# TensorE's instructions in the loop over the mixers' tiles, in the order in which the code writes them

## The chip, the cores and the metric

The kernel runs on one core of a Trainium2 chip. The metric is the device time of one execution in microseconds (us), and the median of several runs is compared. The core has five engines with a queue each: TensorE (PE in the profile; PEld is its weight loads), VectorE (DVE), ScalarE (ACT), GpSimd (POOL) and SyncE (SP), which issues the DMAs here.

## The reference, cut to what matters

One layer of a streaming encoder on 1024 prompt frames and 32 sample frames, with model width 1024: a SwiGLU block, two attention mixers side by side, another SwiGLU block. This case is about the mixers.

```python
def band_attn_a(q, k, v, bias, valid):            # mixer A: 8 heads of 64, 576 keys for each chunk of 64
    s = jnp.einsum('bnqhd,bnkhd->bnhqk', q, k).astype(jnp.float32) * SCALE + bias.astype(jnp.float32)
    s = jnp.where(valid[None, :, None], s, NEG_INF)
    p = jax.nn.softmax(s, axis=-1).astype(v.dtype)
    return jnp.einsum('bnhqk,bnkhd->bnqhd', p, v)
...
o = jnp.concatenate([rmsnorm(oa, group_gains[:WIDTH_A]), rmsnorm(ob, group_gains[WIDTH_A:])], axis=-1) @ w_out
```

Mixer B has 8 query heads on 2 key heads, a window of 192 keys and a learned sink in the softmax. The sample frames attend to cached keys and values.

## The kernel before, in words

Tokens are in three blocks (384, 384, 256 + 32 columns). The first SwiGLU block runs, then the mixers, then the second one. The mixers' stage is a loop over 72 tiles (lines 1229 to 1262), which takes some 407 us of the 2220.7 us span. Tiles 0 to 35 are mixer B (four pairs of heads, each a sample tile `TileS` and eight tiles `TileB` of 128 queries), 36 to 53 are mixer A's pairs of heads 0 and 1, and 54 to 71 its pairs 2 and 3, taken in turn and beginning with those of few keys (128 keys for the first, 640 from the fifth on).

A tile of mixer A has two halves, one for each head. `qk` computes the scores `S` in PSUM with two matmuls (L766, L767): queries and keys are each split into a value rounded to the fast fp32 format (`F32R`) and what is left, and GpSimd makes the split queries `qs` (L738, L739) a tile ahead. Then DVE adds the bias (L769) and finds the maximum (L773), ACT takes the exponential `P` (L781). `tr` transposes `P` on TensorE into `pp` (L798), which ACT or DVE copies out as `PT`; `av` multiplies by the values into `po` (L724; for pairs 2 and 3 also two matmuls on `rden`, L718), which is copied out as `o`. A tile of mixer B is the same with both heads at once: `Sb` (L835, L836), DVE L837 and L839, ACT L846, a scaling (ACT L852, DVE L854), `ppb` (L864), `po`. A sample tile has `Ss`, `Ps`, `pps`, `po`.

PSUM has two buffers for scores (pool `ps2`), three for `pp`, `ppb` and all projections (`ps1`), one for `po` (`psc`).

Beside the tiles the loop runs other work on TensorE: the projections `pq` and `pv` of later heads (24 matmuls each in two pieces, by `fill`), `pkr` and `pkc` (transposed keys), the sums `pss` and `pr` of the group norms (`step`), and from tile 67 on five pieces `wo` of the output projection (`out_piece`). In which order the code writes this is plain from the body of the loop:

```python
for half in range(2):
    scores(n, half)
    tiles[n].tr(half)
    if half == 0 and n:
        tiles[n - 1].av()
    step(1)
    prep_step()
    fill(rate)
```

`scores(n, half)` writes the scores of tile n + 2 up to tile 35, of tile n + 1 from 36 on. The order in which instructions stand in the engines' queues is another matter: a scheduler sets it when the program is built. It takes, by its own estimate of times, what is ready first. `tc.manual_schedule(engines={...})` makes it keep the code's order on the engines named, for what is written inside the block. Buffers and semaphores follow the order that results.

Of the kernel before, what the change touches and what calls it, by code (L numbers as in the profile page):

```python
# [61 lines left out]
KB = 0  # L62
SPLIT = "ggg"
LEAD_B = 2
MANUAL = False
WAIT = 3
PREP = 3
STAGES = ((0, 34), (37, 54))
# [7 lines left out]
def encoder_step(ctx: ExitStack, tc, x_prompt, x_sample, cache_a_k, cache_a_v, cache_b_k, cache_b_v,  # L76
# [1183 lines left out]

    with tc.manual_schedule(engines={mybir.EngineType.PE}) if MANUAL else ExitStack():
        waits[0] = WAIT
# [121 lines left out]
```

## Time and profile before

| | |
|---|---|
| median of 3 runs | 2223.67 us (2222.75 to 2224.6) |
| the profiled execution | 2222.49 us, its span 2220.7 us |
| TensorE busy in the span | 2149.3 us (97%) |
| the other engines | DVE 1218.1 us, ACT 676.3 us, POOL 304.4 us |
| TensorE's mean granted clock | 0.984 |

A span is the time from the first instruction to the last. Matmuls are pipelined, so that a duration in the trace is longer than the time that a matmul takes from the next: a 128x384 matmul is listed with 0.33 us, and the next one starts 0.17 us later. What an instruction costs TensorE is read from starts, not from durations.

### The profile page before, as it was taken

Reading aid. Unit: us, or ns where it says so; the run is one execution under the profiler, and the core shown is the slowest. Engines: PE = TensorE matmul, PEld = TensorE weight load, DVE = VectorE, ACT = ScalarE, POOL = GpSimd, SP = SyncE. Lnnn points to the kernel's source line nnn. Section 1 sums busy time; section 2 is a strip of 40 time slices with the busy share of each in tenths; the row PEclk is TensorE's granted clock in tenths of the full one; section 3 lists DMA queues with packets and bytes.
Section 4 is the critical chain, followed back from the end, with each engine's and each line's share of the span. In section 5 each row is a group of like instructions: output and inputs, shape, how many; then the busy total and the mean of one; then the engine's idle time right before and its main releaser. Section 6 shows DMA issues by size and latency. Waiting matters only on the chain.

```text
span 2220.7 us, 34363 instructions
## 1 busy us (share of the span) xinstructions
PE 2149.3 (97%) x14092; PEld 2074.6 (93%) x14092; DVE 1218.1 (55%) x2314; ACT 676.3 (30%) x1391; POOL 304.4 (14%) x601
## 2 busy tenths in 40 slices
PE   6999999999999999899999899999999999999998
PEld 4999999999999999788788688999999999999998
DVE  5787667865333487566555675775333333333336
ACT  4411111111122253465555663443111111111133
POOL 2100000000000022455323633220000000000000
PEclk9999999999999999899999899999999999999999
DMA  9343334433212352110112121424211111111122
GB/s 323 101 142 115 113 96 124 143 92 112 64 58 70 100 182 81 57 39 21 49 40 60 39 86 67 133 82 117 73 57 39 54 43 38 58 39 57 39 68 80
DMA packets 200753, 186.06 MB, mean 84 GB/s; under 512 B 7724, under 2 KB 169940, under 8 KB 199444
## 3 DMA queue, kind: packets, MB, share of 16 engines
q1 hardware_dynamic: 200596, 183.87, 27.1%
q8 instruction: 110, 1.80, 0.3%
q14 instruction: 47, 0.39, 0.1%
HBM read 164.12 MB, written 22.86 MB: 84 GB/s over the span
## 4 chain that ended last, share of the span: by engine, by line
PE 86%; DVE 6%; DMA 3%; ACT 2%; issue 1%; POOL 1%; SPq 0%; DVEq 0%; ACTq 0%; POOLq 0%
PE dn L329 7%; PE dn L330 7%; PE dn L331 7%; PE gate L330 7%; PE up L330 7%; PE gate L331 7%; PE up L329 7%; PE up L331 7%; PE gate L329 7%; PE po L724 2%; PE pq L329 2%; PE pq L330 2%; PE pq L331 2%; PE pv L675 1%; PE pp L798 1%
## 5 line engine op out<-in xcount | busy, mean ns | idle before, releaser
L307 ACT ACTIVATE w<-raw 128x1024 fp32r<-128x1024 f32 x187 | 196.6, 1058 | 550.2 <-PE gate L330 227.3
L329 PE MATMUL gate<-h_hi,w 128*128 128x384 f32 (+1 forms) x1056 | 341.0, 323 | 4.4 <-DVE sl L555 2.9
L329 PE MATMUL dn<-gg,w 128*128 128x384 f32 (+1 forms) x1056 | 341.7, 325 | 2.3 <-DVE facc L585 2.3
L330 PE MATMUL gate<-h_lo,w 128*128 128x384 f32 (+1 forms) x1056 | 340.5, 322 | 3.5 <-DVE h_lo L450 3.5
L585 DVE TENSOR_TENSOR facc<-dn,facc 128x768 f32<-128x768 f32 (+1 forms) x240 | 212.5, 887 | 233.8 <-PE dn L331 233.8
L331 PE MATMUL gate<-h_hi,w 128*128 128x384 f32 (+1 forms) x1056 | 340.3, 322 | 0.0
L329 PE MATMUL up<-h_hi,w 128*128 128x384 f32 (+1 forms) x1056 | 340.1, 322 | 0.0
L330 PE MATMUL up<-h_lo,w 128*128 128x384 f32 (+1 forms) x1056 | 340.1, 322 | 0.0
L331 PE MATMUL up<-h_hi,w 128*128 128x384 f32 (+1 forms) x1056 | 339.8, 322 | 0.0
L330 PE MATMUL dn<-gg,w 128*128 128x384 f32 (+1 forms) x1056 | 339.8, 322 | 0.0
L331 PE MATMUL dn<-gg,w 128*128 128x384 f32 (+1 forms) x1056 | 339.2, 321 | 0.0
L308 DVE TENSOR_TENSOR w<-raw,w 128x1024 fp32r<-128x1024 f32 x187 | 231.4, 1245 | 129.7 <-ACT w L307 124.5
L372 POOL TENSOR_TENSOR sq<-sq 128x384 f32<-128x384 f32 (+1 forms) x48 | 51.9, 1091 | 1476.7 <-ACT sq L368 1468.3
L555 DVE TENSOR_TENSOR sl<-sl,up 128x384 f32<-128x384 f32 (+1 forms) x132 | 68.3, 518 | 309.4 <-PE up L331 303.6
L329 PEld LDWEIGHTS gate<-h_hi,w 128*128 128x128 f32 x1056 | 198.8, 188 | 5.3 <-DVE sl L555 3.2
L330 PEld LDWEIGHTS gate<-h_lo,w 128*128 128x128 f32 x1056 | 198.8, 188 | 4.1 <-DVE h_lo L450 4.0
L329 PEld LDWEIGHTS dn<-gg,w 128*128 128x128 f32 x1056 | 199.1, 189 | 3.6 <-DVE facc L585 3.5
L330 PEld LDWEIGHTS dn<-gg,w 128*128 128x128 f32 x1056 | 198.9, 188 | 0.1
L331 PEld LDWEIGHTS up<-h_hi,w 128*128 128x128 f32 x1056 | 198.9, 188 | 0.0
L331 PEld LDWEIGHTS gate<-h_hi,w 128*128 128x128 f32 x1056 | 198.9, 188 | 0.0
L330 PEld LDWEIGHTS up<-h_lo,w 128*128 128x128 f32 x1056 | 198.7, 188 | 0.0
L331 PEld LDWEIGHTS dn<-gg,w 128*128 128x128 f32 x1056 | 198.7, 188 | 0.0
(234 smaller groups left out, 3470.7 us busy)
## 6 DMA issues: line engine op xcount, KB each, us to landing
raw<-in_w_mod_dram SPq DMA_DIRECT2D x56, 512.0 KB, 4.0
raw<-in_w_gate_dram SPq DMA_DIRECT2D x54, 512.0 KB, 3.9
raw<-in_w_up_dram SPq DMA_DIRECT2D x54, 512.0 KB, 6.3
raw<-in_w_down_dram SPq DMA_DIRECT2D x54, 512.0 KB, 5.0
raw<-in_w_in_dram SPq DMA_DIRECT2D x18, 512.0 KB, 3.9
wm<-in_w_mod_dram SPq DMA_DIRECT2D x16, 512.0 KB, 6.6
raw<-in_w_out_dram SPq DMA_DIRECT2D x13, 512.0 KB, 4.3
xr<-xs SPq DMA_DIRECT2D x16, 384.0 KB, 5.0
```

The source lines that it names most:

```text
L307: ae.activation(w[0], r, AF.Copy)
L308: ve.tensor_sub(w[1], r, w[0])
L329: te.matmul(ps, w[0][:, k], hi, start=start, stop=False)
L330: te.matmul(ps, w[0][:, k], lo, start=False, stop=False)
L331: te.matmul(ps, w[1][:, k], hi, start=False, stop=stop)
L372: e.tensor_tensor(sq[:, 0, :w], sq[:, 0, :w], sq[:, 1, :w], op=OP.add)
L555: ve.tensor_tensor(sl[:, :w], sl[:, :w], ps[1][:, :w], op=OP.mult)
L585: ve.tensor_tensor(o, ps[:, :, :w], o, op=OP.add)
L675: te.matmul(ps[:n, :256], b, wt[0][:, kk], start=False, stop=k == KT - 1)
L724: te.matmul(po[64 * h:64 * h + 64, :n], vsl(j, h, kn), PT(h, j, kn), start=j == 0, stop=j == nt - 1)
L798: te.transpose(pp[:, j - j0, :], P[:, 128 * j:128 * j + 128], ident)
```

## The change

One constant, which decides whether the loop over the tiles is inside a manual schedule of TensorE.

```diff
 LEAD_B = 2
-MANUAL = False
+MANUAL = True
 WAIT = 3
```

It is used in one place, the line ahead of the loop:

```python
with tc.manual_schedule(engines={mybir.EngineType.PE}) if MANUAL else ExitStack():
```

The other engines' instructions stay the scheduler's to order. TensorE's rows before the loop stand as they did.

The first place is on TensorE near the end of mixer A's pair 1, around the ten `po` of one tile. Before:

```order
L767 MATMUL S<-KS,qs 128x320
L724 MATMUL po<-PT,vt 64x128
L766 MATMUL S<-KS,qs 128x320
L767 MATMUL S<-KS,qs 128x320
L766 MATMUL S<-KS,qs 128x320
L767 MATMUL S<-KS,qs 128x320
L1024 MATMUL pkr<-twice,KS 128x64 x8
L798 MATMUL pp<-ident,P 128x128 x4
L724 MATMUL po<-PT,vt 64x128 x2
L798 MATMUL pp<-ident,P 128x128
L724 MATMUL po<-PT,vt 64x128 x7
```

The same tile's rows with the change, on TensorE:

```order
L766 MATMUL S<-KS,qs 128x320
L767 MATMUL S<-KS,qs 128x320
L766 MATMUL S<-KS,qs 128x320
L767 MATMUL S<-KS,qs 128x320
L798 MATMUL pp<-ident,P 128x128 x5
L724 MATMUL po<-PT,vt 64x128 x10
L1031 MATMUL pkr_12053<-ident,KQs 32x128
```

The ten `po` of a tile stood in three pieces, with scores and transpositions between them; they stand in one piece now. (An fp32 matmul such as `po` is one row here and two instructions in the trace.) Over the whole loop `po` stands in 108 pieces before and in 73 after: 38 and 35 in mixer B's tiles, 39 and 19 in mixer A's pairs 0 and 1, 12 and 8 in the tiles of up to 512 keys that follow, 19 and 11 in the rest.

The second place is on TensorE where mixer A's pairs 2 and 3 begin with tiles of few keys, and the first group norm's sum `pss` is formed. Before:

```order
L766 MATMUL S<-KS,qs 128x128
L767 MATMUL S<-KS,qs 128x128
L724 MATMUL po<-PTs,aux 64x32 x8
L724 MATMUL po<-PTs,vs 64x32 x2
L766 MATMUL S<-KS,qs 128x256
L718 MATMUL po<-ident,rden 64x128 x2
L724 MATMUL po<-PT,vt 64x128
L766 MATMUL S<-KS,qs 128x256
L767 MATMUL S<-KS,qs 128x256 x2
L361 MATMUL pss<-ones,sq 128x1 x3
L798 MATMUL pp<-ident,P 128x128 x3
L724 MATMUL po<-PT,vt 64x128
```

The same place on TensorE with the change:

```order
L724 MATMUL po<-PTs,aux 64x32 x8
L724 MATMUL po<-PTs,vs 64x32 x2
L361 MATMUL pss<-ones,sq 128x1 x3
L766 MATMUL S<-KS,qs 128x128
L767 MATMUL S<-KS,qs 128x128
L798 MATMUL pp<-ident,P 128x128
L766 MATMUL S<-KS,qs 128x256
L767 MATMUL S<-KS,qs 128x256
L798 MATMUL pp<-ident,P 128x128
L718 MATMUL po<-ident,rden 64x128 x2
L724 MATMUL po<-PT,vt 64x128 x2
L766 MATMUL S<-KS,qs 128x256
```

The sum `pss` stood behind three more score tiles and stands ahead of them now; scores and transpositions take turns, one by one.

The third place is on TensorE at the first piece `wo` of the output projection, whose 24 matmuls read the normed outputs `o_hi` and `o_lo`. Before:

```order
L329 MATMUL wo<-o_hi,w 128x384
L798 MATMUL pp<-ident,P 128x128 x5
L718 MATMUL po<-ident,rden 64x128 x2
L724 MATMUL po<-PT,vt 64x128 x10
L330 MATMUL wo<-o_lo,w 128x384
L331 MATMUL wo<-o_hi,w 128x384
```

The same piece on TensorE with the change:

```order
L767 MATMUL S<-KS,qs 128x320
L798 MATMUL pp<-ident,P 128x128 x5
L329 MATMUL wo<-o_hi,w 128x384
L330 MATMUL wo<-o_lo,w 128x384
L331 MATMUL wo<-o_hi,w 128x384
```

The transpositions and the `po` that stood between the first matmul, on `o_hi`, and the second, on `o_lo`, have gone elsewhere; the second follows the first at once.

## Rows read from the trace of the kernel before

**Rows 1.** The page's busy time of each engine and TensorE's granted clock in 40 slices

```profile
PE 2149.3 (97%) x14092; PEld 2074.6 (93%) x14092; DVE 1218.1 (55%) x2314; ACT 676.3 (30%) x1391; POOL 304.4 (14%) x601
...
PEclk9999999999999999899999899999999999999999
```

**Rows 2.** The loop in four stretches: length, busy us of each engine, clock, DMA

```profile
924.00:1076.00 152.00, 147.90 (x1146) 131.33 (x1147) 92.11 (x283) 88.98 (x308) 74.40 (x211) 0.99 0.11 30
1076.00:1222.00 146.00, 140.68 (x1022) 122.21 (x1020) 79.83 (x191) 74.33 (x186) 41.91 (x130) 0.98 0.20 53
1222.00:1261.00 39.00, 30.01 (x201) 22.26 (x199) 26.95 (x86) 22.72 (x65) 26.89 (x63) 0.78 0.18 51
1261.00:1331.00 70.00, 67.80 (x555) 60.08 (x553) 49.52 (x129) 45.65 (x97) 31.75 (x66) 1.00 0.23 69
```

**Rows 3.** TensorE's waits for `po`'s copy in the loop: total us, times, longest

```profile
PE po L718 <- DVE o L729: 2.8, 3, 1.3
```

**Rows 4.** TensorE's timeline at pieces of `po`: start, duration

```profile
1199.33 0.31 PE L767 MATMUL S<-KS,qs 128*128 128x320 f32 x1
1199.57 0.43 PE L724 MATMUL po<-PT,vt 128*64 128x128 f32 x2
1199.93 0.42 PE L766 MATMUL S<-KS,qs 128*128 128x320 f32 x1
1200.18 0.31 PE L767 MATMUL S<-KS,qs 128*128 128x320 f32 x1
1200.33 0.31 PE L766 MATMUL S<-KS,qs 128*128 128x320 f32 x1
...
1209.47 0.44 PE L724 MATMUL po<-PT,vt 128*64 128x128 f32 x4
1209.84 0.33 PE L798 MATMUL pp<-ident,P 128*128 128x128 f32 x1
1210.10 1.09 PE L724 MATMUL po<-PT,vt 128*64 128x128 f32 x14
...
1267.18 0.44 PE L718 MATMUL po<-ident,rden 128*64 128x128 f32 x4 [1.27 <-DVE o L729]
...
1268.42 0.41 PE L766 MATMUL S<-KS,qs 128*128 128x320 f32 x1
```

**Rows 5.** DVE and ACT in the loop by form: what follows mixer B's scores

```profile
L837 DVE TENSOR_TENSOR Sb<-Sb,bias 128x512 f32<-128x512 f32 x28 | 19.6, 699 | 18.1 <-PE Sb L836 17.7
L839 DVE TENSOR_REDUCE nmb<-Sb 128x2 f32<-128x512 f32 x28 | 19.2, 684 | 0.3
...
L846 ACT ACTIVATE Pb<-Sb,nmb 128x256 f32<-128x256 f32 x56 | 26.0, 472 | 5.1 <-DVE nmb L840 4.2 <-DVE denb L849 0.9
L852 ACT ACTIVATE Pb<-Pb,denb 128x256 f32<-128x256 f32 x28 | 14.1, 505 | 5.4 <-DVE denb L849 5.0
```

**Rows 6.** Timeline of TensorE and ACT where mixer A begins

```profile
1077.29 0.66 PE L724 MATMUL po<-PTb,vt 128*64 128x128 f32 x8
1081.21 0.48 PE L766 MATMUL S<-KS,qs 128*128 128x128 f32 x1 [3.27 <-ACT Ps L910]
...
1082.69 0.69 PE L924 MATMUL pps<-ident,Ps 64*128 64x64 f32 x4 [0.25 <-DVE Ps L914]
...
1079.41 1.06 ACT L307 ACTIVATE w<-raw 128x1024 fp32r<-128x1024 f32 x1 [1.14 <-DMA raw<-in_w_in_dram]
```

**Rows 7.** Timeline of TensorE and POOL in the tiles of few keys

```profile
1222.16 0.33 PE L766 MATMUL S<-KS,qs 128*128 128x128 f32 x1
...
1256.02 0.47 PE L766 MATMUL S<-KS,qs 128*128 128x512 f32 x1 [1.28 <-ACT P L781]
...
1230.78 1.00 POOL L374 TENSOR_TENSOR sq<-sq 128x384 f32<-128x384 f32 x1
```

**Rows 8.** Timeline of TensorE and POOL at the first `wo`

```profile
1283.25 0.44 PE L329 MATMUL wo<-o_hi,w 128*128 128x384 f32 x1 [0.64 <-ACT o_hi L1182]
...
1283.34 1.82 POOL L1183 TENSOR_TENSOR o_lo<-z,o_hi 128x768 fp32r<-128x768 f32 x1 [5.00 <-ACT o_hi L1182]
```

## The prediction

> **What bounds the kernel now.** I read the page first: TensorE is busy 97% of the span and no other engine more than 55%, and its granted clock is short of full speed in two of the 40 slices, the 17th and the 23rd [rows 1]. So TensorE's time decides, and a change of its order can give back what it loses between instructions. Then I cut the loop over the tiles, 924 to 1331 us, into four stretches [rows 2]. In mixer B (152 us) and in mixer A's pairs 0 and 1 (146 us) TensorE is listed busy for all but 4.1 and 5.3 us; in the tiles of few keys (39 us) for all but 9.0, at a clock of 0.78; in the rest (70 us) for all but 2.2. That is some 21 us of listed idling in 407. The longest single wait is 3.27 us for ACT's `Ps` [rows 6]; the copy-out of `po` is waited for three times, 2.8 us in all [rows 3]. Listed busy time hides the rest, so I went to the timeline for the starts.
>
> **Pieces of `po`.** Two score matmuls normally start 0.15 us apart (1200.18 to 1200.33) [rows 4]. Around one piece of two `po` instructions the timeline reads: score matmul at 1199.33, `po` at 1199.57, score matmul at 1199.93, the next at 1200.18. `po` starts 0.09 late, keeps TensorE for 0.36, and the second score matmul is 0.10 late: 0.55 us. A whole `po` of 20 takes 1.24 us, 1267.18 to 1268.42. The 18 instructions between the two cases cost 0.88 us, 0.049 each, so two are worth 0.10, and the piece as such costs 0.45. Beside transpositions it is less: four `po` take 0.37 (1209.47 to 1209.84) for 0.20 of work, and the one `pp` behind them 0.26 (1209.84 to 1210.10), where a tenth would do by the pace of `po`'s pairs: 0.17 and 0.16 make 0.33. The smallest reading is that of `po` alone in the first case, 0.36 less 0.10, or 0.26.
>
> The change leaves 73 pieces of 108. Of the 35 that go, 4 are in the tiles of few keys, which I count apart. The other 31 at 0.33 give **-10.2 us**, with -8.1 (0.26) and -14.0 (0.45) as the ends. I take 0.33 because most pieces lie beside transpositions. A rule of the Trainium skill bears on the price: "TensorEngine Tiling (Array Packing)", Tiling Modes, says that a change of tiling mode drains the engine; the trace's rows name 128*64 for `po` and 128*128 for its neighbours, and the cost is there at each change. "TensorE: Matmul & The Clock Gate", Single matmul latency, puts a lone matmul 166 ns over its streaming time at full clock; at two such drains for a piece, an estimate, 31 pieces would be 10.3 us.
>
> **Mixer B, waits.** In the code's order `ppb` of a tile follows the scores of two tiles on. What must happen meanwhile is DVE 0.70 and 0.68, ACT twice 0.47, and a scaling of 0.51 [rows 5]: 2.8 us, and about 4.2 with the small operations between, which I estimate at a half of it more. Between them TensorE does, twice, a `po`, a `ppb`, scores and half a projection. The stretch's 152 us over 36 tiles are 4.2 us a tile, so some 8 us pass; with the gaps and the projections' tail taken off, I count on 6. The cover is 2 us or more, so I cost this at nothing. DVE and ACT are busy 61% and 59% of that stretch [rows 2]; without the cover, each tenth of a us over would cost 3 us in 32 tiles. The three `ps1` buffers come round in similar order in both programs: nothing.
>
> **Where mixer A begins.** TensorE stood 3.27 us for the exponential of the sample tile, which stood on ACT behind a weight conversion that waited for its DMA until 1079.41 [rows 6]. The change keeps ACT's order there, and the DMA is issued after `pkr`'s copy, as before. But in the code's order `pps` comes ahead of one `po` and two score tiles which were done before or during this wait's end. They come after it: a `po` of 0.65 (1077.29 to where the idling begins) and two score matmuls with what else is listed from 1081.21 to 1082.44 (where the 0.25 of idling ahead of `pps` at 1082.69 begins), some 0.6 to 1.2. I take **+1.4 us**, between 0 (if the earlier scores shorten the wait) and 1.9.
>
> **Tiles of few keys.** The old order issued 16 score tiles from 1222.16 to 1256.02 [rows 7], one in 2.26 us. No engine is the bound: of 39 us DVE is busy 26.95, POOL 26.89, ACT 22.72 [rows 2]. It is a chain: scores, bias, maximum, exponential, and then the next scores in the same one of two buffers. The code's order alternates scores and transpositions, and brings each `po` whole (8 pieces for 12); the old one held a score tile back between its two matmuls, and let both buffers wait together. Against it stands `pss`, which now comes ahead of three score tiles and cannot start before POOL's last sum, which ended at 1231.78 (1230.78 and 1.00) [rows 7]. At best the stretch comes down to the busiest engine's 27 us, a gain of 12; at worst three score tiles fall behind the sum, at 2.26 each a loss of 6.8. I take **-4 us**, a little on the gaining side of the middle, since two buffers in turn are worth more than one sum.
>
> **The first `wo`.** Its second matmul needs `o_lo`, which POOL finished at 1285.16 (1283.34 and 1.82), while the first started at 1283.25 [rows 8]. The old order filled this with five `pp` and a whole `po`. Now the matmul waits, and behind it on TensorE wait 22 others, then the next tile's scores. Its price is 1285.16 less some 1283.45: **+1.7 us**, between 0 and 2.4 (with the 0.64 that it already waited).
>
> **Sum.** -10.2 + 1.4 - 4 + 1.7 = -11.1. The profiled execution took 2222.49 us, which gives 2211.4; it lies 1.2 us under the median of the runs, so that I say **2212.6 us**. What this measurement can tell from no change is about 0.2%, 4.4 us: faster is under 2219.2, slower over 2228.1.
>
> **Rivals.**
>
> *The time turns up as waiting.* TensorE gets to its next wait sooner, and that wait ends when it did: buffers copied out by ACT, DMAs. Half the pieces' gain goes and the tiles of few keys give nothing: -5.1 + 1.4 + 1.7 = -2.0, or 2221.7 from the median. For it: the 3.27 us were a DMA's doing. Against it: in the first two stretches TensorE is idle 9.4 us of 298.
>
> *Waits that nothing fills.* TensorE's queue does not pass a waiting matmul: the 3.27 us at 1081.21 show it, with projections at hand. If DVE and ACT take more than the 6 us of cover to return `Pb`, every `ppb` of mixer B stands still, and all behind it. From 0.35 us over the cover the 32 tiles cost 11.1 us and the gain is gone; at 0.6 over they cost 19.2, which with the sum of -11.1 is +8.1, or 2231.8 from the median. Against it: TensorE idles only 4.1 us in that stretch now. The Trainium skill says as much in "TensorE: Matmul & The Clock Gate", Part 2: matmuls stay in program order and only weight loads are pulled ahead; the trace agrees, with no matmul starting in those 3.27 us.
>
> *Both sides turn out well.* Pieces at 0.45 (-14.0), tiles of few keys at their floor (-12), the two losses as taken (+3.1): -22.9, or 2200.8 from the median.
>
> That the order stays as it was is no rival: the rows of the change show it moved.
>
> **How the numbers follow.** The forecast's own case, 2206 to 2219, has a chance of 0.5. The waiting case has 0.25, of which 0.05 lies under 2219.2; the unfilled waits 0.15; the good case 0.1. Faster: 0.5 + 0.1 + 0.05 = 0.65; same 0.2; slower 0.15. The range is 2202 to 2228: it leaves out the slower case, and of the good one the outermost part.
>
> **What would show it.** `po` in 73 pieces in the loop, and the stretches of mixer B and of pairs 0 and 1 shorter by 1 and 7 us with idling about as it was. A wait of `wo` for POOL's `o_lo` of 1.5 to 2.5 us. In the tiles of few keys, score tiles closer than 2.26 us. I am wrong if `ppb` waits for ACT or DVE tile after tile, if `pss` waits over 5 us, or if pieces go and the stretches don't shrink.

## The result: slower by a quarter of a per cent, and the profile after

The median is 2229.28 us (2226.67 to 2232.82, 7 runs) for 2223.67 us before (2220.04 to 2225.31, 7 runs): a ratio of 1.0027, with a 95% interval of 1.0016 to 1.0039. I had said 2212.6 us. The profiled execution took 2226.67 us, the shortest of the seven; its span is 2224.9.

The page first, the two lines that answer to [rows 1], the busy time and TensorE's clock in 40 slices:

```profile
PE 2141.2 (96%) x14092; PEld 2077.5 (93%) x14092; DVE 1218.8 (55%) x2314; ACT 678.7 (31%) x1391; POOL 304.0 (14%) x601
...
PEclk8999999999999999899899799999999999999999
```

TensorE is busy 8.1 us less than before for the same instructions, and the span is 4.2 us longer. The saving is real, then, and something larger was lost. The clock has one more slice under full speed in the loop, and a lower one. To see where, I cut the loop at points that both kernels have: the first scores, and the copies of `po` of the 36th, 54th, 62nd and 72nd tile. The wait where mixer A begins falls into the second row of the kernel before (1081.21 us) and into the first row of the changed one (1075.97), so that the first two rows are best read together. The windows of the kernel before (length, busy us of PE, PEld, DVE, ACT and POOL, clock, DMA share, GB/s; the last row is the whole loop):

```profile
924.30:1078.00 153.70, 149.54 (x1160) 132.18 (x1159) 93.54 (x286) 88.99 (x309) 76.16 (x216) 0.99 0.11 32
1078.00:1223.50 145.50, 139.56 (x1008) 121.77 (x1008) 79.71 (x190) 75.82 (x191) 40.15 (x124) 0.98 0.20 54
1223.50:1261.70 38.20, 29.78 (x198) 21.93 (x197) 26.04 (x88) 21.50 (x62) 27.36 (x65) 0.78 0.14 42
1261.70:1331.90 70.20, 68.09 (x555) 60.77 (x556) 49.82 (x127) 45.38 (x96) 31.28 (x65) 1.00 0.23 69
924.30:1331.90 407.60, 386.98 (x2919) 336.65 (x2919) 249.12 (x687) 231.68 (x655) 174.96 (x469) 0.97 0.17 47
```

The same windows of the changed kernel:

```profile
921.10:1077.90 156.80, 148.09 (x1166) 133.09 (x1165) 96.83 (x292) 93.65 (x318) 77.68 (x220) 0.97 0.15 41
1077.90:1219.30 141.40, 134.20 (x1001) 121.22 (x1001) 78.14 (x183) 73.79 (x183) 41.10 (x120) 0.96 0.17 47
1219.30:1259.80 40.50, 30.12 (x192) 24.02 (x193) 25.18 (x84) 19.37 (x58) 25.96 (x64) 0.62 0.11 31
1259.80:1337.30 77.50, 69.26 (x562) 63.56 (x562) 50.54 (x129) 47.28 (x100) 30.65 (x66) 0.95 0.21 62
921.10:1337.30 416.20, 381.67 (x2919) 341.89 (x2919) 250.68 (x687) 234.10 (x655) 175.39 (x469) 0.93 0.16 46
```

The loop is 8.6 us longer, in one execution of each. TensorE's idle time in it (length less busy time) rose from 20.6 to 34.5 us. The clock has two levels, 2.4 and 1.2 GHz, so the time at the lower one is the length times twice what the clock lacks of 1.00: by the rows, with clocks of two digits, some 26 us before and 59 now. The first 54 tiles took 299.2 us and take 298.2; the last 18 took 108.4 and take 118.0. The 1.0 us is no gain that single executions can tell: in kernels further down with the same order there, the first 54 tiles took 297.8 and 298.4 us in the scheduler's order, and 298.6 to 299.8 in the code's. The 9.6 us of the last 18 are clear of that. After the loop both need 84 us to the second SwiGLU block.

What TensorE waits for in the loop of the changed kernel (us in total, times, longest), against [rows 3] and the single 3.27 us of [rows 6]:

```profile
PE pps L924 <- DVE Ps L914: 8.2, 2, 5.1
PE pss L361 <- POOL sq L374: 8.0, 4, 3.9
PE S L766 <- ACT P L781: 2.6, 3, 2.0
PE po L718 <- DVE o L729: 1.8, 2, 1.3
PE wo L330 <- POOL o_lo L1183: 1.7, 1, 1.7
...
PE wo L329 <- ACT o_hi L1182: 1.4, 1, 1.4
...
PE ppb L864 <- ACT Pb L852: 0.8, 1, 0.8
```

Two names hold 16.2 of the 34.5 us, in six waits: `pps`, the transposed probabilities of a sample tile, and `pss`, the sum of a group norm. The 32 `ppb` of mixer B wait 0.8 us together. So the order does not wait a little everywhere; it waits long at a few places. Some of these places in the timeline of TensorE:

```profile
1070.56 0.28 PE L767 MATMUL S<-KS,qs 128*128 128x128 f32 x1
1075.97 0.68 PE L924 MATMUL pps<-ident,Ps 64*128 64x64 f32 x4 [5.13 <-DVE Ps L914]
...
1221.01 0.43 PE L924 MATMUL pps<-ident,Ps 64*128 64x64 f32 x4 [3.05 <-DVE Ps L914]
...
1228.67 1.44 PE L361 MATMUL pss<-ones,sq 128*128 128x1 f32 x6 [3.92 <-POOL sq L374]
1229.97 0.45 PE L766 MATMUL S<-KS,qs 128*128 128x128 f32 x1
...
1282.22 0.44 PE L329 MATMUL wo<-o_hi,w 128*128 128x384 f32 x1 [1.37 <-ACT o_hi L1182]
1284.37 0.69 PE L330 MATMUL wo<-o_lo,w 128*128 128x384 f32 x1 [1.71 <-POOL o_lo L1183]
...
1320.23 0.83 PE L361 MATMUL pss<-ones,sq 128*128 128x1 f32 x6 [3.13 <-POOL sq L374]
```

Mixer A's entry (the first two rows): TensorE has nothing ahead of `pps` that could run. ACT at the same place:

```profile
1073.01 1.06 ACT L307 ACTIVATE w<-raw 128x1024 fp32r<-128x1024 f32 x1 [2.21 <-DMA raw<-in_w_in_dram]
1073.97 0.69 ACT L910 ACTIVATE Ps<-Ss,nm 64x544 f32<-64x544 f32 x1
```

The exponential `Ps` stands behind a weight rounding that waits for its DMA, as in [rows 6]. TensorE comes there earlier than before, and what it waits for is again held by a rounding and its DMA. And at 1228.67 `pss` waits for GpSimd:

```profile
1226.03 0.98 POOL L372 TENSOR_TENSOR sq<-sq 128x384 f32<-128x384 f32 x1
1227.10 0.45 POOL L739 TENSOR_TENSOR qs<-Q,qs 64x128 fp32r<-64x128 f32 x1
1227.63 0.99 POOL L374 TENSOR_TENSOR sq<-sq 128x384 f32<-128x384 f32 x1
```

GpSimd makes the sum's last two additions with a query split between them, and the scores behind `pss` on TensorE, which ACT and DVE could have worked on, stand too. Last, windows around the wait at mixer A's entry:

```profile
1070.80:1076.00 5.20, 0.07 (x2) 0.03 (x1) 2.57 (x7) 2.99 (x7) 2.25 (x8) 0.65 1.01 256
1076.00:1086.00 10.00, 10.00 (x55) 9.03 (x56) 3.55 (x10) 2.32 (x10) 2.56 (x8) 0.50 0.18 52
1086.00:1096.00 10.00, 10.00 (x68) 9.63 (x67) 4.73 (x9) 4.31 (x10) 0.00 (x0) 1.00 0.01 2
```

Behind the wait TensorE works without a gap for 10 us at half clock, 1.2 GHz, and only then at full speed. The prediction had no term for this, although the kernel before shows it behind its own wait of 3.27 us:

```profile
1081.20:1086.60 5.40, 5.13 (x20) 4.64 (x21) 4.41 (x14) 2.93 (x10) 0.00 (x0) 0.50 0.56 148
```

### The profile page after: what moved, and what is told of

It is laid out like the page before. It is cut to its first block, busy times and chain, and to the rows that moved or that the text cites. A ratio compares the mean times of both kernels' runs of the same rounds, so it can differ in the third digit from the quotient of the medians.

```text
span 2224.9 us, 34373 instructions
## 1 busy us (share of the span) xinstructions
PE 2141.2 (96%) x14092; PEld 2077.5 (93%) x14092; DVE 1218.8 (55%) x2314; ACT 678.7 (31%) x1391; POOL 304.0 (14%) x601
## 4 chain that ended last, share of the span: by engine, by line
PE 84%; DVE 7%; DMA 3%; ACT 2%; issue 2%; POOL 1%; SPq 0%; DVEq 0%; ACTq 0%; POOLq 0%
PE dn L329 7%; PE dn L330 7%; PE dn L331 7%; PE gate L330 7%; PE gate L331 7%; PE up L330 7%; PE up L329 7%; PE up L331 7%; PE gate L329 7%; PE pq L329 2%; PE pq L330 2%; PE pq L331 2%; PE po L724 2%; PE pv L673 1%; PE pv L675 1%
## 5 line engine op out<-in xcount | busy, mean ns | idle before, releaser
L329 PEld LDWEIGHTS dn<-gg,w 128*128 128x128 f32 x1056 | 198.2, 188 | 2.1 <-DVE facc L585 1.4
L331 PEld LDWEIGHTS up<-h_hi,w 128*128 128x128 f32 x1056 | 198.7, 188 | 0.0
L330 PEld LDWEIGHTS dn<-gg,w 128*128 128x128 f32 x1056 | 198.3, 188 | 0.4 <-DVE gg L558 0.3
L329 PEld LDWEIGHTS up<-h_hi,w 128*128 128x128 f32 x1056 | 198.5, 188 | 0.0
```

Of the source, the lines that this page charges most:

```text
L329: te.matmul(ps, w[0][:, k], hi, start=start, stop=False)
L330: te.matmul(ps, w[0][:, k], lo, start=False, stop=False)
L331: te.matmul(ps, w[1][:, k], hi, start=False, stop=stop)
```

## The experiments

The theory after the result: whole pieces do give time, and it is spent, and more, at the named waits and on the half clock behind them. All ratios are to the kernel before, on the same chip as the run; the change itself ran on the first chip only, and stands at 1.0027. A wait or window comes from one execution of a kernel, a ratio from several.

**The order for a part of the loop.** A stack enters the manual schedule at one tile and leaves it at another, for tiles 0 to 35, 36 to 53, and 54 to 71.

```diff
-MANUAL = True
+MAN = (0, 36)
...
+            if n == MAN[1]:
+                part.close()
```

> The code's order for mixer B's 36 tiles alone. Theory (whole pieces of po do give time, and named waits at the sample tiles, the sums pss and wo, with the half clock after them, spend it): mixer B to its last tile had 2.4 us less work at full clock with the change, and mixer A is entered as before: 1 to 4 us faster than before. Rival (pieces are worth nothing, and the code's order merely waits a little everywhere): within 1 us of before, or slower.

> The code's order for mixer A's pairs 0 and 1 alone (tiles 36 to 53). Theory: 20 pieces fewer give some 6.6 us, the sample tile's pps at the entry takes some 2 back: 3 to 6 us faster than before. Rival (pieces are worth nothing): the entry's loss alone, 1 to 3 us slower.

> The code's order for the last 18 tiles alone. Theory: here lie three waits for pss, that of pps, that of the first wo, and most of the half clock: the two stretches were 9.7 us longer with the change, so 7 to 11 us slower than before. Rival (the loss is spread over the loop): 2 to 4 us slower.

Measured: 1.0012 (1.0003 to 1.0020), 1.0032 (1.0020 to 1.0043) and 1.0029 (1.0018 to 1.0041). Each part is slower, and the three add up to far more than the whole. By these ratios the rival of the first expectation held (2.7 us slower), and the other two runs fit neither side: 7.1 us slower where a gain or a loss of at most 3 had been said, and 6.4 us for 7 to 11 or 2 to 4. The windows of the first 54 and the last 18 tiles, for the first kernel:

```profile
922.60:1218.00 295.40, 286.38 (x2168) 253.91 (x2167) 173.28 (x475) 165.70 (x498) 116.31 (x340) 0.98 0.16 43
1218.00:1334.10 116.10, 102.21 (x753) 86.58 (x753) 77.97 (x213) 66.19 (x159) 58.42 (x129) 0.88 0.19 55
```

for the second:

```profile
923.30:1226.20 302.90, 285.01 (x2166) 253.95 (x2165) 175.38 (x475) 166.25 (x500) 118.66 (x340) 0.97 0.16 44
1226.20:1339.80 113.60, 102.83 (x753) 86.72 (x754) 77.31 (x212) 65.95 (x157) 57.78 (x129) 0.88 0.17 50
```

and for the third:

```profile
921.60:1219.40 297.80, 287.51 (x2166) 252.65 (x2165) 172.71 (x476) 164.63 (x499) 117.25 (x340) 0.99 0.15 42
1219.40:1337.30 117.90, 99.50 (x753) 87.47 (x754) 75.57 (x211) 67.22 (x158) 57.62 (x129) 0.86 0.19 55
```

Mixer B alone gains 3.8 us up to the 54th tile (299.2 to 295.4; 2.4 against the third kernel, which has the scheduler's order there too), as the theory said; its gain is gone in the last 18 tiles, which are the scheduler's, and take 116.1 us for 108.4. Pairs 0 and 1 alone lose 3.7 up to the same tile: `pps` at the entry waits 6.38 us there. Their last 18 tiles take 113.6, again in the scheduler's order. The third kernel takes 117.9 in them, the change 118.0. So an order of the scheduler's that begins a little differently loses 5 to 8 us there, where the code's loses 9.6, and at other places: in the first two kernels score tiles wait most, for ACT's `P` (4.7 and 5.5 us for 2.0 before), and `pss` 0.5 us at most. The rival of the third run, a loss spread over the loop, is out by its windows; that the code's order alone makes the last tiles long is out too.

**Sums later.** In the loop, `pss` is written two half tiles later. First with a delay of one step for three ahead of `pr`, so that `pr` stays in place, then with the delay kept, then with the first `wo` a tile later as well.

```diff
-        waits[0] = WAIT
+        waits[:] = LOOP
...
+        for _ in range(waits[1]):
+            yield
         add_up(*behind.pop())
```

`LOOP` is (1, 2) in the first and (3, 2) in the other two; the last has `OUTS = (0,) * 14 + (1,) * 4`.

> The whole loop in the code's order, but the code writes the sums pss two half tiles later (and pr with a delay of one step for three, so that it stands where it stood). Theory: the 8.0 us of waits for POOL's sums become less than 2, and of the 24 us at half clock behind them a good part goes: 4 to 8 us faster than the change, 2221 to 2225. Rival (the wait only moves on, to pr, to the next scores or to wo): within 2 us of the change, and the waits stand under another name.

> As the kernel with the sums later, but pr keeps its delay of three steps and so comes two half tiles later as well. Theory (the waits of 2.6 to 3.2 us for pr there came from the shortened delay): waits for pss under 2 us and for pr under 2, and 3 to 6 us faster than the change. Rival (the chain of the norm is what is late, wherever TensorE asks for it): the wait stands at wo, and the time is within 2 us of the change.

> As the kernel before it, and the first wo comes one tile later (four pieces in the loop for five, the fifth after it). Theory: the waits for o_hi and o_lo, 3.1 us in the change, go too: 5 to 9 us faster than the change, so no slower than before. Rival: the last tiles have less to hide their own chain behind, and no more than 3 us are won.

Measured: 1.0059 (1.0045 to 1.0073), 1.0057 (1.0044 to 1.0070) and 1.0044 (1.0030 to 1.0058): the first two are slower than the change, and the third too by its median, though its interval overlaps the change's. The first kernel's waits:

```profile
PE pr L412 <- DVE ry L343: 9.3, 4, 3.2
...
PE S L770 <- POOL qs L742: 4.2, 3, 2.9
```

`pss` waits some 1.5 us in the loop for 8.0, and the square root's chain on DVE is now waited for at `pr`. With that delay kept, the loop is 413.3 us, shorter than the change's, but what follows it pays. The second kernel after the loop:

```profile
1334.90:1429.10 94.20, 84.46 (x510) 82.65 (x511) 59.24 (x117) 36.28 (x60) 27.95 (x22) 0.91 0.24 82
```

94.2 us for 84.1: the last norms, pushed back a tile, are out of the loop and have little beside them (`pr`, `pss` and `wo` wait some 10 us there, for 4.6 with the change). In all three the wait moves on, as the rivals said, but not to where the second rival had it (its longest new one is at `pp`, 6.5 us), and at a higher price than theirs: 7.1, 6.7 and 3.8 us over the change, where they had it within 2 us or up to 3 us ahead. All three theories, of 3 to 9 us under the change, had the sign wrong.

**The price of a piece.** In pairs 0 and 1 `po` is cut after every two key tiles; the second part follows `scores(n, 1)`, the third `tr(1)`.

```diff
+                if half and n:
+                    next(rest, 0)
                 tiles[n].tr(half)
+                if half and n:
+                    run(rest)
```

> The change, but each po of mixer A's pairs 0 and 1 with more than two key tiles is cut into two or three pieces, with scores and transpositions between them: 20 pieces more, the same matmuls. Theory (a piece costs 0.26 to 0.45 us): 5 to 9 us slower than the change, 2234 to 2238, and the stretch of tiles 36 to 53 longer by as much, with no more waiting. Rival (a piece costs nothing, and the time listed less in that stretch came from elsewhere): within 1 us of the change.

Measured: 1.0039 (1.0024 to 1.0054), 0.12% over the change, with overlapping intervals, so that the time alone doesn't tell the two apart. The window of pairs 0 and 1:

```profile
1079.20:1219.50 140.30, 136.31 (x1001) 119.87 (x1001) 75.17 (x181) 71.60 (x179) 37.84 (x116) 0.97 0.16 43
```

By the trace `po` stands in 34 pieces in this window for 18, so 16 more, not 20. TensorE is busy 2.1 us more (136.31 for 134.20) at a clock of 0.97 for 0.96. That is 2.9 us less at half clock (11.3 to 8.4 us, from clocks rounded to two digits), which would by itself have made the busy time 1.4 us shorter, so the pieces cost some 3.5 us of work, 0.22 each; the rounding of the clocks alone leaves 0.13 to 0.31. The stretch is no longer for it: the idle time fell by 3.2 us. Both sides were half right. A piece costs, by this estimate less than I took; and at this place most of what it costs was waiting before.

**The price of the clock.** Transpositions of the identity, which nobody reads, ahead of four waits ("busy waits": TensorE works where it would stand).

```diff
+            for _ in range(IDLE.get((self.kind, self.p), 0)):
+                te.transpose(pp[:, 6:8, :].rearrange("p a b -> p (a b)"), ident, ident)
```

> The change, and in front of four of the waits (pps of the sample tiles of pairs 0 and 3, pss twice) 32, 18, 24 and 18 transpositions of the identity that nobody reads, so that TensorE works there where it stood. Theory of the clock (the half clock behind the waits is a price of its own, some 24 us at half speed): those stretches at half clock go, and the kernel is 4 to 8 us faster than the change, though it does more. Rival (the waits themselves are the price): within 1.5 us of the change, or up to 3 slower.

> As the kernel with busy waits, and 4 more idle transpositions ahead of each real one of pairs 2 and 3 with up to 512 keys (20 places), and 10 ahead of the first wo. Theory of the clock: the 10 us stretches at half clock that are left between 1226 and 1254 us go, 1 to 4 us faster than the kernel with four busy waits, so at or under the time before. Rival (these tiles are a chain through DVE, ACT and POOL, which TensorE's clock does not shorten, and the added work only delays it): same or up to 4 us slower.

> The code's order for tiles 0 to 53 alone, with the 32 idle transpositions where mixer A begins; the last 18 tiles are the scheduler's again. Theory (up to tile 53 the order gains, and what it lost at mixer A's entry was half clock): 294 us to tile 53 for 299 before, and 2 to 5 us faster than before if the last tiles take what they took (108 us). Rival (the last tiles' time hangs on the scheduler's choices, and no kernel but the one before has had less than 113 us there): the gain is gone there, within 2 us of before or slower.

Measured: 1.0006 (0.9998 to 1.0015), 1.0006 (0.9998 to 1.0015) and 1.0026 (1.0016 to 1.0035). The first kernel's window behind mixer A's entry, its first 54 and last 18 tiles, and its whole loop:

```profile
1077.10:1087.10 10.00, 10.00 (x80) 9.48 (x81) 4.94 (x13) 4.25 (x13) 2.48 (x8) 1.00 0.18 54
...
922.00:1216.10 294.10, 280.76 (x2197) 254.02 (x2196) 175.19 (x474) 165.97 (x497) 118.68 (x340) 0.99 0.16 44
1216.10:1333.20 117.10, 104.56 (x815) 92.13 (x816) 76.24 (x213) 67.94 (x159) 56.69 (x129) 0.88 0.19 53
922.00:1333.20 411.20, 385.33 (x3011) 346.15 (x3011) 251.43 (x687) 233.90 (x655) 175.37 (x469) 0.96 0.16 47
```

The same 10 us behind the wait run at full clock, and with 92 matmuls more the loop is 5.0 us shorter than the change's; 1.0027 to 1.0006 is 4.7 us. So the half clock is a price of its own, most of the loss by the medians. It was paid at mixer A's entry: 4.1 of the 5.0 us are in the first 54 tiles, and the last 18 take 117.1 us for 118.0. In the second kernel the tiles of few keys run at full clock (0.62 in the change, 0.74 in the first kernel), yet take 37.7 us for 40.5 and 40.1, and by the medians the kernel is no faster than the first (its profiled execution is the fastest of its eleven): there the rival held, and a full clock did not shorten the kernel. The third has 294.2 us up to tile 53, as expected, and 121.0 in the last 18 tiles in the scheduler's order; its rival held.

**ACT's place at the entry.** The first two weight roundings after tile 36 are GpSimd's.

```diff
+        if byp[0]:
+            byp[0] -= 1
+            ge.tensor_copy(w[0], r)
+        else:
+            ae.activation(w[0], r, AF.Copy)
```

> The change, with the first two weight roundings after tile 36 on GpSimd for ACT; TensorE's rows in the loop are the same. Theory (the sample tile's exponential stood behind a rounding that waited for its DMA): the wait of 5.1 us for pps falls under 1.5, and 1 to 4 us are won, the rest coming back as a wait for the weights. Rival (the weights' DMA ends the wait in any case): the same idle time, now ahead of pq, and the same time.

Measured: 1.0015 (1.0005 to 1.0025), 2.7 us under the change, though the two intervals overlap. TensorE at the entry:

```profile
1073.16 0.28 PE L773 MATMUL S<-KS,qs 128*128 128x128 f32 x1
1074.92 0.52 PE L930 MATMUL pps<-ident,Ps 64*128 64x64 f32 x4 [1.48 <-DVE Ps L920]
```

The wait is 1.48 us for 5.13, and the first 54 tiles take 293.3 us, 5.9 less than before. So the rounding on ACT held the entry, and not the DMA as such. Part of the gain was lost again in the last 18 tiles: `pss` waits 10.1 us for GpSimd there for 8.0, and they take 119.7 us.

**The same repairs in both orders.** Three repairs where the change waits, each set of them once in the code's order and once in the scheduler's: the norms' sums without GpSimd, the roundings of the run above, and in `wo` the 16 matmuls on `o_hi` ahead of the 8 on `o_lo`. First with sums on TensorE alone (12 one-column matmuls for 3), without and with the two other repairs:

```diff
-        pss = yield from sumsq(src, kts, w, bank, ends)
+        pss = yield from sumsq(src, kts, w, bank, ends, fold)
```

> The change, with the squares of the group norms summed by TensorE alone (12 matmuls on one column for 3, none of GpSimd's three additions a sum, and pss one half tile earlier). Theory (the waits for pss are waits for GpSimd, whose additions stand between its splittings of the queries): waits for pss in the loop 3 us or less for 8.0, and 3 to 6 us faster than the change. Rival (the squares and the output that they read are as late): the same waits, for ACT, and within 1.5 us of the change.

> The same sums on TensorE in the kernel before, in the scheduler's order. Theory (that order hides these sums behind scores): within 2.5 us of before. Rival (GpSimd's additions hold up both orders): 3 us or more faster than before.

> The change with three repairs at the places where it waits: sums on TensorE, the first two weight roundings after tile 36 on GpSimd, and in wo the 16 matmuls on o_hi ahead of the 8 on o_lo. Theory: 3 to 6 us, 2 to 4 and 1 to 2, so 6 to 10 us faster than the change, and no slower than before. Rival (the waits follow the chain to its next place): 3 us or less.

> The same three edits in the kernel before, in the scheduler's order. Theory (what the change loses is at these places, so that without them its whole pieces are left over): within 3 us of before, and 1 to 5 us slower than the same edits in the code's order. Rival (the edits help any order, or the scheduler's order is better for another reason): faster than the same edits in the code's order.

Measured: 1.0035 (1.0023 to 1.0047), 1.0030 (1.0018 to 1.0042), 1.0009 (1.0000 to 1.0018) and 1.0027 (1.0018 to 1.0037). The waits for `pss` fell to 1.1 us in the first kernel's loop, but the sums are dear. Here is half of one (six of the twelve, two instructions each) in the timeline of the fourth, at half clock:

```profile
1226.40 2.72 PE L369 MATMUL pss<-ones,sq 128*128 128x1 f32 x12
```

In the first kernel the last 18 tiles have 118.10 us of TensorE's work for 99.38 in the change. The expectations for sums on TensorE alone, and for the scheduler's order, had missed that price. With three repairs the code's order is 4 us faster than the change, where 6 to 10 had been expected; it is better than the scheduler's by 0.18%, and the two intervals just touch.

Then with the additions on DVE, which cost TensorE nothing:

```diff
+        eng = SQE if bank is None else "vv"
```

> The change with the three repairs, but the squares of the group norms are added up by DVE (no more TensorE work; 12 matmuls for a sum had taken 2.6 us at full clock for 0.65 with three). Theory: the waits for pss halve at least without a price on TensorE, so 2 to 6 us faster than the three repairs with sums on TensorE, and 0 to 5 us faster than before. Rival (DVE is as late as GpSimd): like the three repairs, 0 to 4 us slower than before.

> The same edits in the scheduler's order. Theory (with the waits repaired the code's order is the better one): 2 to 6 us slower than the same edits in the code's order. Rival (the four us between the orders with sums on TensorE were that edit's doing): the same time or faster.

> The code's order with these edits, and 8 and 20 idle transpositions ahead of pps of pairs 0 and 3, where the waits for Ps are left. Theory of the clock: 1 to 4 us faster than without them, and faster than before by 2 to 7 us. Rival: within 1 us of the kernel without them.

Measured: 0.9958 (0.9945 to 0.9972), 0.9967 (0.9955 to 0.9978) and 0.9971 (0.9960 to 0.9981). The loop in the code's order:

```profile
923.70:1327.00 403.30, 374.34 (x2919) 335.56 (x2919) 257.35 (x700) 232.51 (x653) 166.69 (x457) 0.96 0.17 47
```

and in the scheduler's:

```profile
923.00:1328.80 405.80, 389.20 (x2919) 338.93 (x2919) 256.74 (x701) 229.09 (x653) 165.09 (x457) 0.96 0.17 47
```

Both beat the kernel before, 2213.33 and 2214.06 us for 2222.29 on that chip, and by more than the 0 to 5 us that the first expectation gave. Between the orders no difference is left that these runs can tell, and the second expectation (2 to 6 us) missed. The code's order does the same matmuls in 14.9 us less of busy time, and waits (length less busy time) 29.0 us for 16.6. The first 54 tiles took 294.5 us in the code's order and 298.3 in the scheduler's, the last 18 took 108.8 and 107.5:

```profile
1218.20:1327.00 108.80, 93.55 (x753) 82.23 (x754) 81.59 (x226) 67.20 (x158) 44.05 (x115) 0.91 0.19 54
...
1221.30:1328.80 107.50, 99.82 (x753) 85.06 (x753) 81.65 (x227) 66.91 (x158) 44.85 (x115) 0.89 0.20 60
```

What the change had lost there (118.0 us) came back with these repairs. Busy waits on top did not help: the median of the third is 3.1 us above the first's, with overlapping intervals.

## Why the prediction was wrong, by its own steps

The step that failed is the pricing of waits in the last 18 tiles. There the sum had -4 us for the tiles of few keys and -0.9 for the rest (eight pieces and the first `wo`); the change took 2.3 and 7.3 us more. That is 14.5 of the 19.7 us between the -11.1 that I had said and the 8.6 by which the loop grew. The other 5.2 us lie in the first 54 tiles (-6.2 said, -1.0 measured), mostly at mixer A's entry and the half clock behind it.

*What bounds the kernel.* "A change of its order can give back what it loses between instructions": it does. TensorE's busy time in the loop fell by 5.3 us though more of it was at half clock. The step that is missing is that the old order lost that time while it filled waits. With the same repairs, 14.9 us less work stands against 12.4 us more waiting. The two are one account; of the other side I had entered 3.1 us.

*Pieces, -10.2.* They stand in 73 pieces as said. The cut `po` gave some 0.22 a piece where I took 0.33 and had 0.26 as the lowest reading; 31 would be 6.8 us. Mixer B alone, with 3 pieces fewer, gained 2.4 to 3.8 us up to the 54th tile where I had put 1; that other changes from one kind of matmul to another count too is possible, and was not measured apart. The term is probably too large but right in kind, and it is not what failed.

*Mixer B, nothing.* Right: 0.8 us at `ppb`, for 0.9 before.

*Mixer A's entry, +1.4.* The mechanism was right (`pps` ahead of work that used to come first; ACT and the DMA end the wait), the size was not: 5.13 us of waiting for 3.27 and 0.25, and then 10 us at half clock. With the half clock taken away the first 54 tiles take 294.1 us, with the rounding moved 293.3, for 298.2. So 4 to 5 us were lost here that either repair brings back; without them the first 54 tiles gain 5 to 6 us, about what the two terms promised (23 pieces at 0.33 less 1.4 is 6.2). That agreement is in part luck, since the repairs also take away waiting that the 1.4 had allowed for, and a piece gave 0.22. The scheduler's order gained no more than 0.9 there from the same rounding (298.3 for 299.2), so it is not the repair alone.

*Tiles of few keys, -4.* The sign was wrong: 40.5 us for 38.2. I weighed two buffers in turn against one sum and took the gaining side. The sum waited 3.92 us, inside the bound of 6.8 that I gave it; a sample tile's `pps` waited 3.05 us at 1221.01, which I had not looked for although I had costed the same thing 150 us earlier.

*The first `wo`, +1.7.* 1.71 us for `o_lo`, as said; but `o_hi` took 1.37 us, 0.73 more than before. And a later `pss`, at 1320.23, waited 3.13 us, where no term stood at all. The last ten tiles took 77.5 us for 70.2: TensorE stood 6.1 us more in them (8.2 for 2.1), and their clock was 0.95 for 1.00.

*No term for the clock.* The sum prices each wait at its own length. In [rows 2] the mean of 0.78 among the few keys was in sight. The runs with busy waits put the price at some 5 us, most of it at mixer A's entry.

*The rivals.* "The time turns up as waiting" came nearest in mechanism: TensorE got to the entry sooner and stood there until a rounding and its DMA were done. "Waits that nothing fills" had the right sign, and the right reason, a queue that does not pass a waiting matmul; but I looked for it in mixer B's 32 regular tiles, where the cover is good, and not at the single places where the chain is another one: sample tiles, sums, the first output piece.

*What stays open.* In the last 18 tiles the loss of 9.6 us went with the repairs: 108.8 us with them. But the scheduler's order lost there too, 116.1, 113.6 and 121.0 us for 108.4, when only what comes ahead was changed, and not by waits for the sums: in the run with 121.0 TensorE waits 7.7 us for DVE to copy `po` out, for 2.8 before. Why the order before lost so little there, and orders that differ from it only a little lose so much, was not found. Which of the repairs gave how much of the last gain was not run apart either.

## What to carry to other kernels

An order that looks wasteful may be paying for something: before undoing interleaving, list for each piece what it covers, and look first at the irregular places (the first of a kind, a sum, an output's first piece), since regular ones have cover. Price a wait on TensorE with the half clock that the rows show behind earlier waits, not with its own length alone. Where an order waits, moving the waiting instruction later mostly moved the wait here; making its input earlier, on an engine that has time, brought both orders 7 to 9 us under the kernel before, and was worth more than the order.

## What the runs showed of the hardware

At mixer A's entry the clock fell while TensorE stood (0.65 in the 5.2 us of the wait) and stayed at half for 10 us of unbroken work. Behind the wait of 1.67 us that ended at 1208.25 it fell when TensorE was working again: 0.50 from 1208.90 to 1212.30; behind that of 3.13, which ended at 1320.23, likewise from 1321.50 to 1324.90. At the entry 32 useless transpositions, with 1.77 us of waiting left behind them, kept it at 1.00. With the rounding moved to GpSimd the wait there was 1.48 us, and 5 us behind it still ran at half:

```profile
1076.90:1082.00 5.10, 5.10 (x33) 4.41 (x33) 3.48 (x10) 1.14 (x6) 4.73 (x11) 0.50 0.30 76
```

So the length of a wait alone did not decide what came behind it. Among the tiles of few keys a full clock for one of 0.62 went with 2.8 us of 40.5, no more. GpSimd rounded a 128x1024 weight in 1.04 us (mean of two), ACT in 1.06.
